# Stick-breaking attention on one core: z for a pair of heads at a time, one head in each half of the PE array's rows, in place of z for one head over all rows

## Chip, cores and metric

The kernel runs on one core of a Trainium2 chip. The metric is device time in microseconds (us) of one execution; the figure compared is the median of several runs, and one further execution is profiled.

## The reference

One layer of a streaming encoder trunk: 1024 tokens, width 1024, all in float32. It has three parts, each followed by a layer norm over `alpha*x + y`: self-attention, cross-attention into a memory of 256 tokens (4 heads), and a gated MLP with a short convolution. Only the first part matters here. It has 16 heads of width 64 and works on blocks of 128 queries:

```python
z = einsum('bhtd,bhsd->bhts', q[start:end], k[:end]) * 64 ** -0.5
earlier = arange(end)[None, :] < arange(start, end)[:, None]
log_keep = where(earlier, log_sigmoid(-z), 0.0)
csum = cumsum(log_keep, axis=-1)
w = where(earlier, exp(log_sigmoid(z) + csum[..., -1:] - csum), 0.0)
out = einsum('bhts,bhsd->bhtd', w, v[:end])
```

The output of the 16 heads is multiplied by a 1024 x 1024 matrix (`mix_wo`), added to `alpha*x` and normalized.

## The kernel before

**Numbers as pairs.** Every product is made to float32 accuracy from fp32r operands: each operand is split into hi (a cast) and lo (the rest, by a subtraction); `split` (L77) does that on two engines that its caller names. `mm3` (L100 to L103) makes a product as three matmuls, hi by hi, hi by lo, lo by hi, into one PSUM accumulator.

**PSUM.** Eight banks, two each under the tags acc (projections), pv, z and tp (L65 to L75).

**Projections.** x arrives transposed in eight tiles of 128 features and is split into xh and xl (L392 to L396). `proj_steps` (L182) is a generator: a step is one `mm3` of 512 columns. Head h takes one 128 x 1024 weight (`wqk`: 64 columns of q, 64 of k), two halves of 512 tokens, eight steps each; after it comes half of the values of a pair of heads (`wv`). `weights` (L164) loads a weight into wraw (two buffers) and splits it on POOL into whl (two buffers). The first head's queries and keys and the first pair's values are made ahead of the loop, as x arrives (L383 to L406).

**Queries and keys of a head.** `qk_out` (L131) copies the accumulator to pj on ACT, casts both halves on ACT into q1 (rows 0 to 63: hi of q) and k1 (rows 64 to 127: hi of k), subtracts the lo parts on POOL into the other halves of q1 and k1, and has two transfers on the SP queue build q2, which is q1 with its halves exchanged. So k1 holds lo over hi, q1 hi over lo and q2 lo over hi: q1 by k1 gives hi-lo and lo-hi, q2 by k1 gives lo-lo and hi-hi. Two 128-row matmuls thus make z.

**Attention.** `z_piece` (L207) makes a block of 128 queries by S = 128 to 1024 keys, in one or two pieces of at most 512 columns: two matmuls into a z bank (L215, L216), then a sigmoid on ACT into sig (L217); over the block one mask on POOL (L219) and one product scan on DVE (L222). `t_piece` (L224) transposes up to four 128 x 128 pieces of sig on TensorE into tp and splits them into wT (ACT and DVE). `pv_piece` (L236) multiplies wT by the differences of the values (vst); its lo part has 64 output columns. `o_piece` (L248) adds the ends and, for the odd head of a pair, sends two blocks of oT to DRAM (o_d) on the SP queue.

**Order.** `attention` (L266) takes half a head at a time ("quad": 18 of the 36 blocks). While the transposes and products of one quad are issued, the z pieces of the next are put between them in proportion, and `spend` (L271) draws steps of `other_steps` by a planned PE time: 24 steps per head, with an offset LEAD of -5, none within the last head. The compiler's scheduler then orders each engine's instructions by this program order as priority, among those it holds ready. `LAG` keeps three wT ahead of their products.

**What the other steps are.** After all projections, `other_steps` (L373) closes the pool of xh and xl, yields until the attention says that z of the last even head is under way, closes att3 (tiles of the even heads) and goes on with `mem_steps` (L340): mh and ml of the memory, then vacc (values of the memory, weights xv) and kacc (keys, weights xk), with the eight parts of `mix_wo` (wo, L365) loaded and split in between. xv and xk come into buffers of their own (xraw, two), wo and the memory into wraw. Then `out_ln` (L478) multiplies by wo (yacc) and normalizes; its residual tiles come from the pool rp, opened in `mem_steps`.

Of the kernel before, what the change touches and what calls it, by code (L numbers as in the profile page):

```python
# [27 lines left out]
P = 128  # L28
D = 1024
# [12 lines left out]
def trunk(ctx, tc, out, xT, xn, memT, wqk, wv, wo, xq, xk, xv, xo, up, cw, dn, lng, lnb):  # L42
# [80 lines left out]
    def qk_tiles(h):  # L123
        return [(att2 if h % 2 else att3).tile([P, T], R, name=f"{n}{h % 2}") for n in ("q1", "q2", "k1")]

    def evacuate(acc, n=512):
        pj = att.tile([P, 512], F32, name="pj", bufs=3)
        nc.scalar.copy(out=pj[:, :n], in_=acc)
        return pj[:, :n]

    def qk_out(qk, acc, ns):  # L131

        q1, q2, k1 = qk
        pj = evacuate(acc)
        for dst, r in ((q1, slice(0, 64)), (k1, slice(64, 128))):
            nc.scalar.copy(out=dst[r, ns], in_=pj[r])
        nc.gpsimd.tensor_tensor(out=q1[64:128, ns], in0=pj[0:64], in1=q1[0:64, ns].bitcast(F32), op=ALU.subtract)
        nc.gpsimd.tensor_tensor(out=k1[0:64, ns], in0=pj[64:128], in1=k1[64:128, ns].bitcast(F32), op=ALU.subtract)
        nc.sync.dma_start(out=q2[0:64, ns].bitcast(F32), in_=q1[64:128, ns].bitcast(F32))
        nc.sync.dma_start(out=q2[64:128, ns].bitcast(F32), in_=q1[0:64, ns].bitcast(F32))  # L140

    def v_out(pair, acc, n):
        vst, vend = pair
# [7 lines left out]
        dv = att.tile([P, 512], F32, name="pj", bufs=3)  # L151
# [20 lines left out]
    def vst_tile(pr):  # L172

        p = att2 if pr % 2 else att3
        return p.tile([P, KT, 2, 128], R, name=f"vst{pr % 2}"), p.tile([P, NTB], F32, name=f"vend{pr % 2}")

    heads = {}
    pairs = {}

    ready = {0}  # L180

    def proj_steps():  # L182

        for h in range(1, H):
            w = weights(wqk[h])
            qk = heads[1] if h == 1 else qk_tiles(h)
            for n, ns in halves():
                acc = acc_tile(name="qkacc")
                for kt in range(KT):
                    proj_part(w, acc, kt, ns)  # L190
                    yield
                qk_out(qk, acc, ns)
            heads[h] = qk
            ready.add(h)
            pr = (h + 1) // 2
            if pr < H // 2:
                n = 1 - h % 2
                w = weights(wv[pr])
                if n == 0:
                    pairs[pr] = pairs[1] if pr == 1 else vst_tile(pr)  # L200
                acc = acc_tile(name="vtacc")
                for kt in range(KT):
                    proj_part(w, acc, kt, slice(512 * n, 512 * n + 512))
                    yield
                v_out(pairs[pr], acc, n)

    def z_piece(h, i, sig):  # L207

        q1, q2, k1 = heads[h]
# [9 lines left out]
        nc.gpsimd.affine_select(out=sig[:, S - P:S], in_=sig[:, S - P:S], pattern=[[-1, P]], base=-1,  # L219
                                channel_multiplier=1, compare_op=ALU.is_ge, fill=1.0)  # L220
        kr = sig[:, :S][:, ::-1]
        nc.vector.tensor_tensor_scan(out=kr, data0=kr, data1=kr, initial=1.0, op0=ALU.mult, op1=ALU.bypass)  # L222
# [25 lines left out]
    def o_piece(h, d, pv):  # L248
        r = slice(64 * (h % 2), 64 * (h % 2) + 64)
        if h % 2 == 0 and d == 3:  # L250
            state["oT"] = att.tile([P, NTB, P], F32, name="oT", bufs=2)
# [10 lines left out]
    ATT_PE = 0.109 * 36 * 2 + 0.218 * 20  # L262
    LEAD = -5
    LAG = 3

    def attention(others):  # L266
        seq = [(h, q) for h in range(H) for q in (((3, 0), (2, 1)) if h < H - 1 else ((2, 1), (0, 3)))]
        clock = {"t": 0.0, "n": 0}
        pend = []

        def spend(dt):  # L271
            clock["t"] += dt
            if clock["t"] > (H - 1) * ATT_PE:
                return
# [4 lines left out]
        def z_steps(h, quad, sigs):  # L279
            while h not in ready:  # L280
                next(others)
                clock["n"] += 1
            sig = att.tile([P, 18 * P], F32, name="sig", bufs=2)
            c = 0
            for d in quad:
                for i in (2 * d, 2 * d + 1):
                    sigs[i] = sig[:, c:c + P * (i + 1)]
                    c += P * (i + 1)
                    z_piece(h, i, sigs[i])
                    yield 0.109 * (i + 1)  # L290

        def flush():
            h, d, b0, wT, pv = pend.pop(0)
            pv_piece(h, d, b0, wT, pv)
            if b0 == 2 * d:
                o_piece(h, d, pv)
            return 0.436

        def t_steps(h, quad, sigs):
            for d in quad:  # L300
                pv = None
                for b0 in range(0, 2 * d + 2, 2):
                    wT = t_piece(sigs, d, b0)
                    yield 0.109 * (4 if b0 < 2 * d else 3)
                    if pv is None:
                        pv = pv_tile((P, 2, P), name="pv")
                    pend.append((h, d, b0, wT, pv))
                    if len(pend) > LAG:
                        yield flush()

        spend(0.0)
        sigs = {}
        for dt in z_steps(*seq[0], sigs):
            spend(dt)
        for g, hq in enumerate(seq):
            nxt = {}
            zs = z_steps(*seq[g + 1], nxt) if g + 1 < len(seq) else iter(())
            tz = tt = 0.0
            for dt in t_steps(*hq, sigs):
                tt += dt  # L320
                spend(dt)
                while tz < tt * 18 / 34:
# [7 lines left out]
            if seq[min(g + 2, len(seq) - 1)][0] == H - 1:  # L330
# [9 lines left out]
    def mem_steps():  # L340
        mp = mem_c.enter_context(pool(name="memp", bufs=1, side="right", reuse_waits="tile"))
        wop = mem_c.enter_context(pool(name="wop", bufs=1, side="right", reuse_waits="tile"))
        state["rp"] = mem_c.enter_context(pool(name="rp", bufs=2, side="right", reuse_waits="tile"))
# [19 lines left out]
        for dq in range(KT):  # L363
            w = load_w(xk[dq], "pool", "pool", raw=mp.tile([P, 1024], F32, name="xraw", bufs=2)).rearrange("p a (k m) -> p a k m", k=KT)
# [17 lines left out]
    heads[0], heads[1], pairs[0], pairs[1] = qk_tiles(0), qk_tiles(1), vst_tile(0), vst_tile(1)  # L382
    w0, wv0 = [], []  # L383
    for k2 in range(KT // 2):
        for src, lst in ((wqk[0], w0), (wv[0], wv0)):
# [5 lines left out]
        for kt in (2 * k2, 2 * k2 + 1):  # L391
            xr = att.tile([P, 18 * P], F32, name="sig", bufs=2)  # L392
# [3 lines left out]
    w0, wv0 = (w[1].rearrange("p a (k m) -> p a k m", k=KT) for w in (w0, wv0))  # L396
    accs = [acc_tile(name="qkacc") for n in range(2)]
    vccs = [pv_tile(name="vtacc") for n in range(2)]
    for kt in range(KT):
        for w, cc in ((w0, accs), (wv0, vccs)):  # L400
            for n, ns in halves():
                proj_part(w, cc[n], kt, ns)
    for n, ns in halves():
        qk_out(heads[0], accs[n], ns)
    for n, ns in halves():
        v_out(pairs[0], vccs[n], n)  # L406
# [98 lines left out]
    att_c.close()  # L505
    h1c = ExitStack()
# [7 lines left out]
    with ExitStack() as c1:  # L514
        lnp = c1.enter_context(pool(name="ln1", bufs=1, side="right", reuse_waits="tile"))
        gb = load_ln(lnp, 0)
        for k, i in enumerate((4, 5, 2, 3, 0, 1, 6, 7)):
            out_ln(k, i, o_d, wts, xn, state["rp"], gb, h1_d, h1_evac)
# [489 lines left out]
```

## Time and profile before

| | |
|---|---|
| median of 3 runs | 1557.54 us (1556.81 to 1560.26) |
| the profiled execution | 1561.96 us |
| its span, first to last instruction | 1560.2 us |
| mean granted TensorE clock | 0.991 of full speed |
| PE, PEld busy | 1511.1 us (97%), 1261.4 us (81%) |
| DVE, ACT, POOL busy | 1090.8 us (70%), 701.6 us (45%), 676.9 us (43%) |
| instructions of PE | 7508 matmuls, 7508 weight loads |
| DMA | 191.00 MB, mean 122 GB/s |

Engines: PE is TensorE's matmul, PEld its weight load (which overlaps PE), DVE VectorE, ACT ScalarE, POOL GpSimd, SP SyncE, which here issues transfers. L215 is line 215. A share of busy time is a mean over stages with different limits, so a stage is read by itself. Matmuls are pipelined: one starts before the one ahead of it has ended, so the time that a matmul takes from its neighbours is the distance between starts. "a <-b" after an idle time names what ended it.

### The profile page before, as it was taken

The page shows a single profiled execution, that of the slowest core. Times are in us where ns is not written, and L with a number is a line of the kernel's source. Part 1 is how long each engine was busy: PE and PEld are TensorE (multiplying, and loading weights), DVE is VectorE, ACT ScalarE, POOL GpSimd, SP SyncE. Part 2 cuts the span into 40 slices and gives each one's busy share as a digit, 9 for nine tenths or more (in the row PEclk, how much of TensorE's full clock was granted, in tenths as well). Part 3 has the DMA queues.
Part 4 walks back from the last instruction along what each step waited for, and adds up shares of the span by engine and source line. Part 5 has one row for each costly group of instructions (what it writes and reads, how often), then busy time and mean ns, then how long its engine had stood idle before and what let it go on. Part 6 is the DMA issues. An engine that isn't in the chain of part 4 may idle for free.

```text
span 1560.2 us, 21007 instructions
## 1 busy us (share of the span) xinstructions
PE 1511.1 (97%) x7508; PEld 1261.4 (81%) x7508; DVE 1090.8 (70%) x1504; ACT 701.6 (45%) x1309; POOL 676.9 (43%) x627
## 2 busy tenths in 40 slices
PE   7999999999988999999999989999999999989997
PEld 5888888888877888888888867888888888778876
DVE  3466666676769836645437899777777777868896
ACT  4455565565567522123332355444444444444551
POOL 4775566556558730255401253222444543501042
PEclk9999999999998999999999999999999999999999
DMA  5322222122236443334234415443466662944631
GB/s 172 85 59 65 65 56 70 48 62 68 61 97 191 163 137 135 113 118 128 82 109 168 135 65 174 147 154 126 133 151 149 151 146 96 355 142 160 195 105 61
DMA packets 95352, 191.00 MB, mean 122 GB/s; under 512 B 11408, under 2 KB 33040, under 8 KB 95248
## 3 DMA queue, kind: packets, MB, share of 16 engines
q1 hardware_dynamic: 75760, 143.52, 29.2%
q0 software_dynamic: 11136, 27.27, 7.4%
q10 hardware_dynamic: 8352, 18.88, 3.6%
q8 instruction: 59, 0.97, 0.3%
q14 instruction: 45, 0.37, 0.1%
HBM read 146.63 MB, written 57.67 MB: 131 GB/s over the span
## 4 chain that ended last, share of the span: by engine, by line
PE 81%; DVE 6%; POOL 5%; issue 3%; DMA 3%; ACT 1%; SPq 0%; POOLq 0%; DVEq 0%; ACTq 0%
PE yacc L101 4%; PE yacc L102 4%; PE yacc L103 4%; PE qkacc L101 4%; PE qkacc L103 4%; PE qkacc L102 4%; PE mb L101 3%; PE mb L103 3%; PE mb L102 3%; PE tp L231 3%; PE y L102 3%; PE y L103 3%; PE y L101 3%; PE mc L102 2%; PE mc L103 2%
## 5 line engine op out<-in xcount | busy, mean ns | idle before, releaser
L222 DVE TENSOR_TENSOR_SCAN sig<-sig 128x896 f32<-128x896 f32 (+7 forms) x128 | 196.4, 1541 | 75.5 <-POOL sig L219 56.5
L87 POOL TENSOR_TENSOR whl<-wraw,whl 128x512 fp32r<-128x512 f32 (+2 forms) x97 | 172.7, 1791 | 134.2 <-ACT whl L79 132.7
L85 DVE TENSOR_TENSOR wT<-tp,wT 128x512 fp32r<-128x512 f32 (+1 forms) x160 | 98.8, 628 | 63.1 <-ACT wT L79 61.9
L79 ACT CAST whl<-wraw 128x512 fp32r<-128x512 f32 (+3 forms) x113 | 82.3, 739 | 123.7 <-PE y L103 39.1
L79 ACT CAST wT<-tp 128x512 fp32r<-128x512 f32 (+1 forms) x160 | 86.5, 546 | 105.4 <-PE tp L231 102.0
L448 POOL TENSOR_TENSOR rs<-rs,mhalf 128x1 f32<-128x1 f32 x24 | 22.3, 930 | 224.5 <-DVE rs L447 224.5
L217 ACT ACTIVATE sig<-z 128x384 f32<-128x384 f32 (+2 forms) x192 | 92.1, 495 | 49.9 <-PE z L216 48.8
L219 POOL TENSOR_SCALAR_AFFINE_SELECT sig<-sig 128x128 f32<-128x128 f32 x128 | 60.2, 474 | 119.7 <-ACT sig L217 112.0
L101 PE MATMUL qkacc<-xh,whl 128*128 128x512 f32 x256 | 103.2, 403 | 8.0 <-ACT xh L79 6.5
L101 PE MATMUL mb<-b_t,ws 128*128 128x512 f32 x264 | 104.7, 397 | 2.0 <-ACT b_t L79 1.0
L102 PE MATMUL y<-whl,aop 128*128 128x512 f32 x264 | 103.7, 393 | 1.1 <-DVE whl L85 1.0
L103 PE MATMUL mb<-b_t,ws 128*128 128x512 f32 x264 | 103.9, 394 | 0.0
L103 PE MATMUL qkacc<-xh,whl 128*128 128x512 f32 x256 | 102.0, 400 | 1.9 <-POOL whl L87 1.9
L102 PE MATMUL mb<-b_t,ws 128*128 128x512 f32 x264 | 103.3, 391 | 0.0
L102 PE MATMUL qkacc<-xl,whl 128*128 128x512 f32 x256 | 102.3, 399 | 0.0
L103 PE MATMUL yacc<-wo,whl 128*128 128x512 f32 x256 | 100.8, 394 | 0.0
L102 PE MATMUL yacc<-wo,whl 128*128 128x512 f32 x256 | 100.8, 394 | 0.0
L101 PE MATMUL yacc<-wo,whl 128*128 128x512 f32 x256 | 100.4, 393 | 0.3 <-ACT whl L79 0.3
L103 PE MATMUL y<-whl,aop 128*128 128x512 f32 x264 | 99.7, 391 | 0.0
L79 ACT CAST ws<-wt 128x512 fp32r<-128x512 f32 x88 | 54.5, 621 | 99.3 <-PE mb L103 53.9
L231 PE MATMUL tp<-ident,sig 128*128 128x128 f32 x576 | 89.4, 275 | 8.8 <-DVE wT L85 8.8
L83 POOL TENSOR_SCALAR whl<-wraw 128x512 fp32r<-128x512 f32 (+2 forms) x74 | 55.3, 760 | 88.3 <-PE qkacc L103 31.3
(222 smaller groups left out, 4393.9 us busy)
## 6 DMA issues: line engine op xcount, KB each, us to landing
wraw<-in_up SPq DMA_DIRECT2D x22, 512.0 KB, 3.6
wr<-in_up SPq DMA_DIRECT2D x22, 512.0 KB, 3.6
u_d<-in_dn SPq DMA_DIRECT2D x44, 256.0 KB, 5.5
float<-g_d POOLq DMA_DIRECT2D x44, 256.0 KB, 6.4
wraw<-u_d SPq DMA_DIRECT2D x44, 256.0 KB, 2.9
g_d<-gate SPq DMA_DIRECT2D x20, 512.0 KB, 2.9
q<-q SPq DMA_DIRECT2D x64, 128.0 KB, 2.2
h_d<-r SPq DMA_DIRECT2D x32, 256.0 KB, 2.1
```

The costliest lines, as they stand in the source:

```text
L79: nc.scalar.copy(out=hi, in_=src)
L83: nc.gpsimd.tensor_scalar(out=hi, in0=src, scalar1=1.0, scalar2=0.0, op0=ALU.mult, op1=ALU.add)
L85: nc.vector.tensor_tensor(out=lo, in0=src, in1=hi.bitcast(F32), op=ALU.subtract)
L87: nc.gpsimd.tensor_tensor(out=lo, in0=src, in1=hi.bitcast(F32), op=ALU.subtract)
L101: nc.tensor.matmul(o, lhsT=lh, rhs=rh, start=first, stop=False, skip_group_check=more)
L102: nc.tensor.matmul(o, lhsT=lh, rhs=rl, start=False, stop=False, skip_group_check=more)
L103: nc.tensor.matmul(o, lhsT=ll, rhs=rh, start=False, stop=last, skip_group_check=more)
L217: nc.scalar.activation(out=sig[:, a:b], in_=z[:, :b - a], func=AF.Sigmoid, scale=-0.125)
L219: nc.gpsimd.affine_select(out=sig[:, S - P:S], in_=sig[:, S - P:S], pattern=[[-1, P]], base=-1, channel_multiplier=1, compare_op=ALU.is_ge ...
L222: nc.vector.tensor_tensor_scan(out=kr, data0=kr, data1=kr, initial=1.0, op0=ALU.mult, op1=ALU.bypass)
L231: nc.tensor.transpose(out=tp[:, k], in_=sigs[2 * d + u][:, P * j:P * j + P], identity=ident)
L448: nc.gpsimd.tensor_tensor(out=rs, in0=rs, in1=mhalf, op=ALU.pow)
```

## The change

`qk_tiles`, `qk_out`: for a pair of heads there are now four tiles, q hi, q lo, k hi, k lo, each with the even head in rows 0 to 63 and the odd head in rows 64 to 127. The weights are cut accordingly (`wq`, `wk`: 128 columns for a pair). The accumulator is split straight from PSUM by ACT and DVE. `z_piece` makes the pieces of both heads together: hi by hi, hi by lo, lo by hi, each as two matmuls of 64 rows, one per head, into the two z banks; then two sigmoids, and for each head a mask and a scan.

```diff
     def qk_out(hl, acc, ns):
-        q1, q2, k1 = qk
-        pj = evacuate(acc)
-        for dst, r in ((q1, slice(0, 64)), (k1, slice(64, 128))):
-            nc.scalar.copy(out=dst[r, ns], in_=pj[r])
-        nc.gpsimd.tensor_tensor(out=q1[64:128, ns], in0=pj[0:64], in1=q1[0:64, ns].bitcast(F32), op=ALU.subtract)
-        nc.gpsimd.tensor_tensor(out=k1[0:64, ns], in0=pj[64:128], in1=k1[64:128, ns].bitcast(F32), op=ALU.subtract)
-        nc.sync.dma_start(out=q2[0:64, ns].bitcast(F32), in_=q1[64:128, ns].bitcast(F32))
-        nc.sync.dma_start(out=q2[64:128, ns].bitcast(F32), in_=q1[0:64, ns].bitcast(F32))
+        split(acc, hl[0][:, ns], hl[1][:, ns])
...
+        rows = slice(0, 64), slice(64, 128)
         for (a, b) in reversed([(0, c), (c, S)] if c < S else [(0, S)]):
-            z = z_tile()
-            nc.tensor.matmul(z[:, :b - a], lhsT=q1[:, tb], rhs=k1[:, a:b], start=True, stop=False)
-            nc.tensor.matmul(z[:, :b - a], lhsT=q2[:, tb], rhs=k1[:, a:b], start=False, stop=True)
-            nc.scalar.activation(out=sig[:, a:b], in_=z[:, :b - a], func=AF.Sigmoid, scale=-0.125)
+            zs = [z_tile() for r in rows]
+            for n, (x, y) in enumerate(((0, 0), (0, 1), (1, 0))):
+                for z, r in zip(zs, rows):
+                    nc.tensor.matmul(z[:, :b - a], lhsT=q[x][r, tb], rhs=k[y][r, a:b], start=n == 0, stop=n == 2)
+            for z, sig in zip(zs, sigs):
+                nc.scalar.activation(out=sig[:, a:b], in_=z[:, :b - a], func=AF.Sigmoid, scale=-0.125)
...
+    Z_PE, T_PE, V_PE = 0.171, 0.109, 0.436
+    QUAD_PE = 18 * Z_PE + 2 * (18 * T_PE + 5 * V_PE)
+    FIRST, PACE = 40, 25
...
-            while clock["n"] < LEAD + 24 * clock["t"] / ATT_PE:
-                clock["n"] += 1
-                next(others, None)
+            while clock["n"] < FIRST + PACE * clock["t"] / QUAD_PE:
+                other()
...
-        state["rp"] = mem_c.enter_context(pool(name="rp", bufs=2, side="right", reuse_waits="tile"))
...
-                w = load_w(xv[n, k2], "act", "pool", raw=mp.tile([P, 1024], F32, name="xraw", bufs=2)).rearrange("p a (k m) -> p a k m", k=2)
+                w = load_w(xv[n, k2], "act", "pool").rearrange("p a (k m) -> p a k m", k=2)
...
-            w = load_w(xk[dq], "pool", "pool", raw=mp.tile([P, 1024], F32, name="xraw", bufs=2)).rearrange("p a (k m) -> p a k m", k=KT)
+            w = load_w(xk[dq], "pool", "pool").rearrange("p a (k m) -> p a k m", k=KT)
```

Around it:

- A quad is now 18 blocks of both heads of a pair (16 quads in all, before 32 of one head). `proj_steps` makes, per pair, the values after queries and keys; the first pair's values are no longer made ahead of the loop but its queries and keys are, and 40 other steps are drawn over the first quad's z, then 25 per quad, to the end.
- A product waits in the program for the values of its pair (`v_ready`).
- The tiles of queries and keys alternate by pair between att3 and att2; the values' tiles all lie in att2, so att3 closes once z of the last but one pair is made.
- Buffers: sig 4 (before 2, now two per quad), pj 2 (3), oT 1 (2). The buffers xraw are gone: xv and xk come into wraw. The pool rp is opened after the attention's pools are closed.

## Rows read from the trace of the kernel before

**Rows 1.** The page's first line.
```profile
span 1560.2 us, 21007 instructions
```
**Rows 2.** Windows: length, then busy time (count) by engine, PE clock, DMA share, GB/s.
```profile
0.00:31.00 31.00, 24.45 (x95) 19.46 (x96) 11.97 (x17) 11.89 (x19) 11.62 (x23) 1.00 0.63 203
31.00:60.00 29.00, 26.11 (x110) 20.14 (x109) 6.34 (x7) 13.62 (x27) 25.05 (x27) 0.94 0.31 78
60.00:460.00 400.00, 397.68 (x2321) 343.85 (x2320) 264.31 (x309) 225.97 (x510) 237.04 (x266) 1.00 0.23 64
460.00:563.00 103.00, 89.96 (x584) 79.42 (x583) 83.53 (x78) 62.52 (x124) 81.66 (x52) 0.95 0.56 178
563.00:1560.00 997.00, 972.91 (x4407) 798.50 (x4405) 724.63 (x1094) 387.58 (x631) 321.57 (x261) 0.99 0.46 139
```
**Rows 3.** Waits of PE, 60 to 460 us: total us, times, longest.
```profile
PE tp L231 <- DVE wT L85: 1.4, 2, 0.8
PE qkacc L101 <- DVE pj L152: 0.9, 1, 0.9
```
**Rows 4.** Timeline of PE, 203 to 205 us: start, duration, instruction.
```profile
203.20 0.34 PE L216 MATMUL z<-k,q 128*128 128x384 f32 x1
203.38 0.28 PE L244 MATMUL pv<-wT,vst 128*128 128x256 f32 x1
...
204.18 0.39 PE L215 MATMUL z<-k,q 128*128 128x512 f32 x1
204.41 0.39 PE L216 MATMUL z<-k,q 128*128 128x512 f32 x1
204.63 0.28 PE L244 MATMUL pv<-wT,vst 128*128 128x256 f32 x1
204.75 0.28 PE L246 MATMUL pv<-wT,vst 128*64 128x256 f32 x1
204.87 0.40 PE L101 MATMUL qkacc<-xh,whl 128*128 128x512 f32 x1
```
**Rows 5.** The same view, 213 to 214 us.
```profile
213.64 0.22 PE L215 MATMUL z<-k,q 128*128 128x128 f32 x1
213.70 0.28 PE L216 MATMUL z<-k,q 128*128 128x128 f32 x1
```
**Rows 6.** Groups by form, ACT, 0 to 455 us: busy us, mean ns | idle before.
```profile
L217 ACT ACTIVATE sig<-z 128x512 f32<-128x512 f32 x68 | 40.3, 602 | 11.0 <-PE z L216 10.6
...
L136 ACT CAST q<-pj 64x512 fp32r<-64x512 f32 x30 | 17.6, 622 | 2.3 <-PE z L215 2.1
```
**Rows 7.** The same view for POOL.
```profile
L138 POOL TENSOR_TENSOR k<-pj,k 64x512 fp32r<-64x512 f32 x30 | 51.6, 1730 | 1.8
...
L137 POOL TENSOR_TENSOR q<-pj,q 64x512 fp32r<-64x512 f32 x30 | 42.1, 1414 | 12.2 <-ACT q L136 9.1 <-issue 1.9
```
**Rows 8.** The same view for DVE.
```profile
L152 DVE TENSOR_TENSOR pj<-vT,vtacc 128x512 f32<-128x512 f32 x16 | 11.0, 687 | 15.6 <-POOL k L138 10.2 <-ACT vT L149 5.2
```
**Rows 9.** Timeline of PE, 35 to 36 us; in brackets the idle time before.
```profile
35.60 0.50 PE L103 MATMUL qkacc<-xh,whl 128*128 128x512 f32 x1 [0.88 <-POOL whl L87]
```
**Rows 10.** DMA issues, 450 to 566 us: size of each, median us to landing.
```profile
xraw<-in_xv SPq DMA_DIRECT2D x8, 512.0 KB, 4.5
wraw<-in_wo SPq DMA_DIRECT2D x8, 512.0 KB, 3.7
xraw<-in_xk SPq DMA_DIRECT2D x8, 512.0 KB, 4.6
...
o_d<-oT SPq DMA_DIRECT2D x16, 64.0 KB, 3.5
```
**Rows 11.** Groups by form, 455 to 563 us.
```profile
L87 POOL TENSOR_TENSOR whl<-xraw,whl 128x1024 fp32r<-128x1024 f32 x16 | 43.3, 2707 | 7.7 <-ACT whl L79 7.0
L85 DVE TENSOR_TENSOR wo<-wraw,wo 128x1024 fp32r<-128x1024 f32 x8 | 17.3, 2164 | 0.1
...
L79 ACT CAST wo<-wraw 128x1024 fp32r<-128x1024 f32 x8 | 8.4, 1049 | 2.1 <-DMA wraw<-in_wo 1.9
```

More of the change, by code (lines that the diff above doesn't have):

```diff
@@ L39, with trunk @@
 EPS = 1e-5
-def trunk(ctx, tc, out, xT, xn, memT, wqk, wv, wo, xq, xk, xv, xo, up, cw, dn, lng, lnb):
+def trunk(ctx, tc, out, xT, xn, memT, wq, wk, wv, wo, xq, xk, xv, xo, up, cw, dn, lng, lnb):
     nc = tc.nc
@@ L172, in vst_tile @@
     def vst_tile(pr):
[L174 to L180, printed above, removed]
-    def proj_steps():
-        for h in range(1, H):
-            w = weights(wqk[h])
-            qk = heads[1] if h == 1 else qk_tiles(h)
+        return (att2.tile([P, KT, 2, 128], R, name=f"vst{pr % 2}"), att2.tile([P, NTB], F32, name=f"vend{pr % 2}"))
+    qks, pairs = {}, {}
+    ready, v_ready = {0}, set()
+    def proj_steps():
+        for pr in range(H // 2):
+            if pr:
+                qks[pr] = qk_tiles(pr)
+                for src, hl in zip((wq, wk), qks[pr]):
+                    w = weights(src[pr])
+                    for n, ns in halves():
+                        acc = acc_tile(name="qkacc")
+                        for kt in range(KT):
+                            proj_part(w, acc, kt, ns)
+                            yield
+                        qk_out(hl, acc, ns)
+                ready.add(pr)
+            w = weights(wv[pr])
+            pairs[pr] = vst_tile(pr)
             for n, ns in halves():
-                acc = acc_tile(name="qkacc")
+                acc = acc_tile(name="vtacc")
                 for kt in range(KT):
@@ L191, in proj_steps, with z_piece @@
                     yield
[L192 to L204, printed above, removed]
                 v_out(pairs[pr], acc, n)
-    def z_piece(h, i, sig):
-        q1, q2, k1 = heads[h]
+            v_ready.add(pr)
+    def z_piece(pr, i, sigs):
+        q, k = qks[pr]
         tb = slice(P * i, P * i + P)
@@ L249, in o_piece @@
         r = slice(64 * (h % 2), 64 * (h % 2) + 64)
-        if h % 2 == 0 and d == 3:
-            state["oT"] = att.tile([P, NTB, P], F32, name="oT", bufs=2)
+        if state.get("pair") != h // 2:
+            state["pair"] = h // 2
+            state["oT"] = att.tile([P, NTB, P], F32, name="oT", bufs=1)
         vend = pairs[h // 2][1]
@@ L260, in o_piece, with other, z_steps @@
                 nc.sync.dma_start(out=o_d[i][:, h // 2], in_=state["oT"][:, i])
-    ATT_PE = 0.109 * 36 * 2 + 0.218 * 20
-    LEAD = -5
+    Z_PE, T_PE, V_PE = 0.171, 0.109, 0.436
+    QUAD_PE = 18 * Z_PE + 2 * (18 * T_PE + 5 * V_PE)
+    FIRST, PACE = 40, 25
     LAG = 3
     def attention(others):
-        seq = [(h, q) for h in range(H) for q in (((3, 0), (2, 1)) if h < H - 1 else ((2, 1), (0, 3)))]
+        seq = [(pr, q) for pr in range(H // 2) for q in (((3, 0), (2, 1)) if pr < H // 2 - 1 else ((2, 1), (0, 3)))]
         clock = {"t": 0.0, "n": 0}
         pend = []
+        def other():
+            clock["n"] += 1
+            next(others, None)
         def spend(dt):
             clock["t"] += dt
-            if clock["t"] > (H - 1) * ATT_PE:
-                return
-            while clock["n"] < LEAD + 24 * clock["t"] / ATT_PE:
-                clock["n"] += 1
-                next(others, None)
[L279 to L283, printed above, removed]
+            while clock["n"] < FIRST + PACE * clock["t"] / QUAD_PE:
+                other()
+        def z_steps(pr, quad, sigs):
+            while pr not in ready:
+                other()
+            tiles = [att.tile([P, 18 * P], F32, name="sig", bufs=4) for hh in range(2)]
             c = 0
@@ L286, in z_steps @@
                 for i in (2 * d, 2 * d + 1):
-                    sigs[i] = sig[:, c:c + P * (i + 1)]
+                    for hh in range(2):
+                        sigs[hh][i] = tiles[hh][:, c:c + P * (i + 1)]
                     c += P * (i + 1)
-                    z_piece(h, i, sigs[i])
-                    yield 0.109 * (i + 1)
+                    z_piece(pr, i, [sigs[hh][i] for hh in range(2)])
+                    yield Z_PE * (i + 1)
         def flush():
             h, d, b0, wT, pv = pend.pop(0)
+            while h // 2 not in v_ready:
+                other()
             pv_piece(h, d, b0, wT, pv)
@@ L296, in flush, with t_steps @@
                 o_piece(h, d, pv)
[L297 to L316, printed above, removed]
+            return V_PE
+        def t_steps(pr, quad, sigs):
+            for hh in range(2):
+                for d in quad:
+                    pv = None
+                    for b0 in range(0, 2 * d + 2, 2):
+                        wT = t_piece(sigs[hh], d, b0)
+                        yield T_PE * (4 if b0 < 2 * d else 3)
+                        if pv is None:
+                            pv = pv_tile((P, 2, P), name="pv")
+                        pend.append((2 * pr + hh, d, b0, wT, pv))
+                        if len(pend) > LAG:
+                            yield flush()
+        sigs = {}, {}
+        for k, dt in enumerate(z_steps(*seq[0], sigs)):
+            while clock["n"] < FIRST * (k + 1) / 4:
+                other()
+        for g, pq in enumerate(seq):
+            nxt = {}, {}
             zs = z_steps(*seq[g + 1], nxt) if g + 1 < len(seq) else iter(())
             tz = tt = 0.0
-            for dt in t_steps(*hq, sigs):
+            for dt in t_steps(*pq, sigs):
                 tt += dt
                 spend(dt)
-                while tz < tt * 18 / 34:
+                while tz < tt * 0.42:
                     dz = next(zs, None)
@@ L329, in attention @@
                 spend(dz)
[L330 removed]
+            if seq[min(g + 2, len(seq) - 1)][0] == H // 2 - 1:
                 state["att3 done"] = True
@@ L379, in other_steps @@
         yield from mem_steps()
-    heads[0], heads[1], pairs[0], pairs[1] = qk_tiles(0), qk_tiles(1), vst_tile(0), vst_tile(1)
-    w0, wv0 = [], []
+    qks[0] = qk_tiles(0)
+    w0, w1 = [], []
     for k2 in range(KT // 2):
-        for src, lst in ((wqk[0], w0), (wv[0], wv0)):
+        for src, lst in ((wq[0], w0), (wk[0], w1)):
             cs = slice(2 * P * k2, 2 * P * k2 + 2 * P)
@@ L395, in trunk @@
                 split(xr[:, ns], xh[:, kt, ns], xl[:, kt, ns])
-    w0, wv0 = (w[1].rearrange("p a (k m) -> p a k m", k=KT) for w in (w0, wv0))
-    accs = [acc_tile(name="qkacc") for n in range(2)]
-    vccs = [pv_tile(name="vtacc") for n in range(2)]
+    w0, w1 = (w[1].rearrange("p a (k m) -> p a k m", k=KT) for w in (w0, w1))
+    accs = [acc_tile(name="qkacc") for n in range(2)], [pv_tile(name="qkacc") for n in range(2)]
     for kt in range(KT):
-        for w, cc in ((w0, accs), (wv0, vccs)):
+        for w, cc in zip((w0, w1), accs):
             for n, ns in halves():
                 proj_part(w, cc[n], kt, ns)
[L403 to L406, printed above, removed]
+    for hl, cc in zip(qks[0], accs):
+        for n, ns in halves():
+            qk_out(hl, cc[n], ns)
     state = {"att3 done": False}
@@ L505, in trunk @@
     att_c.close()
+    rp1 = mem_c.enter_context(pool(name="rp", bufs=2, side="right", reuse_waits="tile"))
     h1c = ExitStack()
@@ L517, in trunk @@
         for k, i in enumerate((4, 5, 2, 3, 0, 1, 6, 7)):
-            out_ln(k, i, o_d, wts, xn, state["rp"], gb, h1_d, h1_evac)
+            out_ln(k, i, o_d, wts, xn, rp1, gb, h1_d, h1_evac)
     mem_c.close()
```

25 lines of the change are left out of this document (14 added, 11 removed).

## Prediction

> **What bounds the kernel now.** The page's first line gives the span, 1560.2 us [rows 1]; the execution it belongs to took 1561.96 us, 1.8 us lie around the span, and the median of the runs is 1557.54 us, 4.4 us less. I sum against the profiled execution and move the same difference to the median.
>
> The windows come next, because the change touches only the self-attention [rows 2]. See five stretches. In 0 to 31 us x arrives and is split. In 31 to 60 us the first head is made ready: PE is busy 26.11 of 29 us at a granted clock of 0.94. From 60 to 460 us projections and attention run together: PE 397.68 of 400 us, DVE 264, ACT 226, POOL 237; TensorE alone is the bound. From 460 to 563 us the last three heads run beside the memory steps: PE 89.96 of 103 us, clock 0.95, DVE 83.53, POOL 81.66; here PE waits. The 997 us after that hold nothing the diff edits except where one small pool is opened.
>
> A busy PE need not be a PE at its peak, so I read who it waited for: in 60 to 460 us 2.3 us in all, two entries [rows 3]. So a matmul microsecond removed there is a microsecond of the kernel.
>
> The price of a matmul is the distance between two starts, not its duration [rows 4, 5]: 512 columns 0.23 us (204.18, 204.41, 204.63), 384 columns 0.18 (203.20, 203.38), 256 columns 0.12 (204.63, 204.75), 128 columns 0.06 (213.64, 213.70). The duration of the 512-wide one, 0.39 us, is 0.16 longer than that distance: the tail of one lies under the next.
>
> **Part 1, z by 64-row matmuls.** For one head z_piece makes 12 pieces (5 of 512 columns, 3 of 384, 3 of 256, 1 of 128), two matmuls each. One pass over them costs 5 x 0.231 + 3 x 0.176 + 3 x 0.119 + 0.058 = 2.10 us (the third digit is the mean over the stretch; with the two digits of the rows it is 2.11), so 16 heads x 2 passes = 67.1 us. Afterwards each pair makes three passes for two heads. If the two halves of the rows run side by side, 8 pairs x 3 passes x 2.10 = 50.4 us: **-16.8**. If they run one after the other it is six passes, 100.7 us: +33.6. No row of this trace has a matmul of fewer than 128 rows. The nearest is the product with 64 columns (128*64), which follows and precedes full ones at the ordinary distance of 0.12 us [rows 4], so a partly used array costs nothing extra in itself. I take side by side, since the two operands lie in different rows and the results in different banks.
>
> The Trainium skill (TensorE: Matmul & The Clock Gate, Measured speedup vs the span model) gives 3.07 times for four 32-row tiles of 512 columns, 77% of the ideal. By that share z would cost 65.5 us, an estimate from that page, and the sum below would be +3.7 instead of -11.4; no run here shows it.
>
> Weights: every matmul loads its own 128 columns. At 128 wide the distance is 0.06 us with a load in each [rows 5], so a couple of loads can't take less than about 0.12, and the one 128-wide piece gains nothing from lying side by side: 3 x 0.058 x 8 = **+1.4** (0 to 1.4). Wider pieces cover two loads.
>
> Banks: z has two PSUM banks. Before, one piece filled one, and the next piece had the other. Now one pair of pieces fills both, and the next pair waits for two sigmoids, which ACT does one after the other, 0.602 us at 512 wide [rows 6]. Four of the 12 pieces are the second half of a block over 512 columns and come right behind the first. PE need not stand still, since projections are ready, but head A's bank is free 0.6 us before B's, so A's matmuls may be put ahead of B's and the two no longer lie beside each other. One lost overlap per such piece costs a pass: (0.176 + 3 x 0.231) x 8 = **+7.0**; none lost 0, all three lost +20.9. I take one, since 0.6 us is under three passes of 0.23.
>
> **Part 2, queries and keys split from PSUM.** Gone, 32 times: the copy to pj stays as the copy to hi, but two half copies on ACT (0.62 each), two subtractions on POOL (1.41 and 1.73) and two transfers on SP go; one subtraction on DVE comes, near 0.687, the row that also reads PSUM [rows 6 to 8]. ACT loses some 40 us, POOL 100, SP 64 issues, DVE gains 22. All of it lies under PE in 60 to 460 us, where DVE goes from 264 to some 285 of 400. On the path: **0**. Bounds: -2.3, all PE waits of rows 3; +4, if the bank that DVE now frees 0.69 us later than ACT did is missed in one of five of the 28 halves. What waits on DVE behind such a subtraction is the lo split of wT, and on that PE's transposes.
>
> One oT instead of two adds a wait: the first add of the next pair on DVE waits for o_d to be written, 3.5 us from issue to landing [rows 10]. Between the adds lie four pv pieces; a head has ten and takes some 30 us (176 matmuls and transposes of the 2321 in 400 us), so 12 us cover it. Cost 0; uncovered, it would hold the same lo splits.
>
> **Part 3, start.** POOL no longer does q and k between the two halves of the second weights, for whose lo part PE stood 0.88 us [rows 9]. In 31 to 60 us 2.9 us are idle and 6% of clock is missing, 1.7 us: at most -4.6. The first split of the new weights still waits for the buffers, so I take **-3** (-4.6 to 0).
>
> **Part 4, end.** As before, the memory steps can begin when the last but one pair's z is made, with three heads to go; that moment moves with what parts 1 and 3 save. But xv and xk lose their own raw buffers and share two wraw buffers with wo. A buffer is held from issue until split: xv 4.5 + 1.0 + 2.7, xk 4.6 + 1.0 + 2.7, wo 3.7 + 1.0 + 2.2 us [rows 10, 11] (xk's cast on POOL taken like ACT's). Eight of each, over two buffers: 8 x 23.4 / 2 = 94 us, in a stretch of 103. It fits by 9 us. Against that, POOL has no q and k of the last heads, and wo's subtractions no longer crowd in ahead of the scans on DVE. I take **0**, between -13 (all idle time of PE there) and +12 (each of 24 turns 1 us later). The residual's buffers open later; r is needed only after 48 yacc matmuls, 11 us, so 0.
>
> **Sum:** -16.8 + 1.4 + 7.0 + 0 - 3 + 0 = -11.4. Profiled execution 1550.6, median **1546**.
>
> **Rivals.**
> - **A, the forecast**: 1546, own range 1530 to 1556. For: PE is the bound for 400 us. Against: no 64-row matmul in the trace. Chance 0.64.
> - **B, slower: PE empties at each change between whole and halved rows.** Some 12 groups a pair go in and out: 192 changes. What a full emptying could cost is the tail that now lies under the next matmul, 0.16 us [rows 4]: +31, 1577. It decides from 11.4 / 192 = 59 ns. Against: between full and 64-column matmuls no such cost stands in the rows. 0.10. The Trainium skill (TensorEngine Tiling (Array Packing), Key Properties) says that a change of tiling mode drains the engine; if 128x64 is such a mode, rows 4 speak against the cost, and for 64 rows no run here shows it yet.
> - **C, slower: the halves run one after the other.** z +33.6 in place of -8.4, start -3: +31, 1588. It is also the case that the change doesn't do what it says. 0.06.
> - **D: all overlap lost in the second halves.** +13.9 on the forecast: +2.5, 1560. For: both sigmoids are on one queue. 0.10.
> - **E: the wraw turns bind the end.** +12: 1558. For: only 9 us of room. Against: POOL is freer. 0.10.
>
> **How the numbers follow.** A difference of 0.2%, 3.1 us, is about what a measurement of this kernel can tell from no change. A is faster: 0.64. D and E are within it, less a little that lies beyond: 0.17. B, C and that rest: 0.19. The range leaves out C, B beyond 135 ns per change, and the corner where z keeps all its overlap and the end loses most of its idle time: 1526 to 1572.
>
> **What would show it.** Right: three z lines of 64 rows, 576 matmuls in all, starts of a couple a few ns apart and 0.23 us from couple to couple; 60 us to the last projection shorter by some 9 us; POOL under half busy there; yacc starting near 551 us. Wrong: couples 0.46 us apart (C); a gap of over 60 ns before and after each group (B); three matmuls of one head in a row (D); PE or vacc and kacc waiting for wraw transfers, with the stretch after the last projection over 110 us (E).

## The result: 2.7% slower

The changed kernel takes a median of 1600.19 us (1596.29 to 1602.88, four runs), the kernel before 1557.57 us in the same comparison: ratio 1.0269, 95% interval 1.0239 to 1.0298, or +42.6 us. The forecast was 1546, its range ended at 1572. The profiled execution took 1596.29 us (before 1561.96); it is the lowest of the four, so the windows below hold 34.3 us of the loss.

The page's first lines of the kernel after:

```profile
span 1594.5 us, 20976 instructions
...
PE 1550.1 (97%) x7700; PEld 1254.9 (79%) x7700; DVE 1097.5 (69%) x1536; ACT 667.3 (42%) x1245; POOL 537.6 (34%) x535
```

POOL lost 139 us of work and PE gained 39 us of busy time. The windows of after, cut at the last projection (480 us) and at the first yacc (598 us), with the columns of [rows 2]:

```profile
0.00:31.00 31.00, 24.31 (x98) 19.88 (x99) 14.78 (x20) 13.20 (x21) 13.82 (x26) 1.00 0.62 204
31.00:60.00 29.00, 29.00 (x138) 21.30 (x137) 13.68 (x12) 10.03 (x21) 14.79 (x18) 1.00 0.17 55
60.00:480.00 420.00, 420.00 (x2406) 326.74 (x2405) 264.87 (x328) 193.04 (x446) 118.54 (x184) 1.00 0.11 32
480.00:598.00 118.00, 103.08 (x658) 86.55 (x656) 78.77 (x84) 63.85 (x128) 69.16 (x48) 0.94 0.49 156
598.00:1594.00 996.00, 973.74 (x4404) 800.45 (x4404) 725.37 (x1095) 387.15 (x631) 321.32 (x261) 0.99 0.45 140
```

Against [rows 2]: the start is better, as forecast (31 to 60 us: 29.00 busy at clock 1.00, before 26.11 at 0.94). Yacc begins at 598 us instead of 563, and the rest is as long as before (996 and 997 us). So the loss lies between 60 and 598 us. And in 60 to 480 us PE is busy for all of 420.00 us at full clock, and no wait is listed there: most of the loss is inside a PE that counts as busy, and no view of waits can show it.

It shows in the distance between starts. The timeline of PE in after (x2: two matmuls that start together, one per head, which is a couple; z matmuls with no other matmul between them are a group):

```profile
204.39 0.39 PE L102 MATMUL vtacc<-xl,whl 128*128 128x512 f32 x1
204.62 0.40 PE L103 MATMUL vtacc<-xh,whl 128*128 128x512 f32 x1
204.94 0.50 PE L208 MATMUL z<-kh,qh 64*128 64x512 f32 x2
205.28 0.39 PE L208 MATMUL z<-kl,qh 64*128 64x512 f32 x2
205.50 0.39 PE L208 MATMUL z<-kh,ql 64*128 64x512 f32 x2
205.82 0.38 PE L238 MATMUL pv<-wT,vst 128*128 128x256 f32 x1
206.04 0.28 PE L240 MATMUL pv<-wT,vst 128*64 128x256 f32 x1
206.16 0.28 PE L238 MATMUL pv<-wT,vst 128*128 128x256 f32 x1
```

By [rows 4] 512 columns take 0.23 us from start to start and 256 take 0.12. Read down: 0.32 into the first couple (0.09 too much), 0.34 to the second (0.11), 0.22 to the third (as it should be), 0.32 to the first full matmul (0.09), 0.22 behind 256 columns (0.10), then 0.12 again. The couples do lie side by side, and inside the group their price is that of one matmul. But each passage between 128-row and 64-row matmuls costs twice, once ahead of the first instruction of the new kind and once behind it. The medians over the groups that stand beside no transpose (some 90 of 125) are 96 + 105 ns going in and 94 + 107 ns going out, **0.40 us for a group**; the same measure on the kernel before gives at most 3 ns.

The weight loads show what is lost. The timeline of PEld, after, same place:

```profile
204.39 0.19 PEld L103 LDWEIGHTS vtacc<-xh,whl 128*128 128x128 f32 x1
204.94 0.19 PEld L208 LDWEIGHTS z<-kh,qh 64*128 64x128 f32 x2 [0.36 <-ACT wT L79]
205.05 0.19 PEld L208 LDWEIGHTS z<-kl,qh 64*128 64x128 f32 x2
205.28 0.19 PEld L208 LDWEIGHTS z<-kh,ql 64*128 64x128 f32 x2
205.82 0.19 PEld L238 LDWEIGHTS pv<-wT,vst 128*128 128x128 f32 x1 [0.35 <-issue]
```

The load for the matmul at 204.62 is made at 204.39, under the matmul ahead. The first 64-row load is not made until 204.94, when the 0.23 us of the last full matmul are over, and so again on the way out at 205.82. (The ACT named beside the 0.36 had ended at 204.83. It is not what the load stood for: where such a cast is named, 14 times, the matmul comes 94 ns late in the median, and where none is named, 49 times, 91 ns.) In the kernel before, the load for z at 204.18 comes at 204.06, under its neighbour:

```profile
204.06 0.19 PEld L215 LDWEIGHTS z<-k,q 128*128 128x128 f32 x1
204.18 0.19 PEld L216 LDWEIGHTS z<-k,q 128*128 128x128 f32 x1
```

A second thing shows in the order on PE: 96 groups of three couples became 125. 71 are whole, 33 are one head's three matmuls alone, the others are fragments; 226 of the 288 couples lie side by side. One such lone head, timeline of PE in after:

```profile
226.76 0.40 PE L101 MATMUL qkacc<-xh,whl 128*128 128x512 f32 x1
227.09 0.49 PE L208 MATMUL z<-kh,qh 64*128 64x512 f32 x1
227.42 0.39 PE L208 MATMUL z<-kl,qh 64*128 64x512 f32 x1
227.66 0.39 PE L208 MATMUL z<-kh,ql 64*128 64x512 f32 x1
227.98 0.51 PE L102 MATMUL qkacc<-xl,whl 128*128 128x512 f32 x1
```

It pays the passage in and out (0.33 and 0.32 instead of 0.23) and has nothing beside it. That is the broken overlap of rival D, with B's price on top.

### The profile page after: what moved, and what is told of

It reads as the page before. It is cut to its first block, busy times and chain, and to the rows that moved or that the text cites. A ratio compares the mean times of both kernels' runs of the same rounds, so it can differ in the third digit from the quotient of the medians.

```text
span 1594.5 us, 20976 instructions
## 1 busy us (share of the span) xinstructions
PE 1550.1 (97%) x7700; PEld 1254.9 (79%) x7700; DVE 1097.5 (69%) x1536; ACT 667.3 (42%) x1245; POOL 537.6 (34%) x535
## 4 chain that ended last, share of the span: by engine, by line
PE 83%; DVE 5%; DMA 4%; POOL 4%; issue 2%; ACT 1%; SPq 0%; POOLq 0%; ACTq 0%; DVEq 0%
PE z L208 5%; PE qkacc L101 4%; PE qkacc L102 4%; PE qkacc L103 4%; PE tp L225 4%; PE yacc L101 4%; PE yacc L102 4%; PE yacc L103 4%; PE mb L101 3%; PE mb L103 3%; PE mb L102 3%; PE y L102 3%; PE y L103 3%; PE y L101 2%; PE pv L238 2%; PE mc L101 2%
## 5 line engine op out<-in xcount | busy, mean ns | idle before, releaser
L87 POOL TENSOR_TENSOR whl<-wraw,whl 128x1024 fp32r<-128x1024 f32 (+2 forms) x99 | 192.0, 1950 | 145.6 <-ACT whl L79 144.3
L216 DVE TENSOR_TENSOR_SCAN sig<-sig 128x1024 f32<-128x1024 f32 (+7 forms) x128 | 183.5, 1460 | 50.3 <-ACT sig L210 36.0
L79 ACT CAST whl<-wraw 128x512 fp32r<-128x512 f32 (+3 forms) x121 | 90.5, 760 | 132.7 <-PE yacc L103 40.9
L210 ACT ACTIVATE sig<-z 128x384 f32<-128x384 f32 (+3 forms) x192 | 86.5, 490 | 100.9 <-PE z L208 99.9
L213 POOL TENSOR_SCALAR_AFFINE_SELECT sig<-sig 128x128 f32<-128x128 f32 x128 | 46.2, 373 | 214.5 <-ACT sig L210 213.8
L83 POOL TENSOR_SCALAR whl<-wraw 128x512 fp32r<-128x512 f32 (+2 forms) x68 | 64.9, 966 | 138.6 <-PE qkacc L103 53.2
```

Source lines behind the costliest of these rows:

```text
L79: nc.scalar.copy(out=hi, in_=src)
L83: nc.gpsimd.tensor_scalar(out=hi, in0=src, scalar1=1.0, scalar2=0.0, op0=ALU.mult, op1=ALU.add)
L87: nc.gpsimd.tensor_tensor(out=lo, in0=src, in1=hi.bitcast(F32), op=ALU.subtract)
```

## The experiments

Two theories were set against each other first. **Theory 1**: overlap is real, and the passages between row counts eat it (with groups broken up, since the two banks come free one at a time). **Rivals**: the halves don't overlap; or the loss comes from another part, the new start, the split from PSUM or the shared raw buffers. All ratios are against the kernel before.

**e1: z with full rows, two matmuls per head, all else as changed.** The sums of both heads land in each bank and one of the three products is missing.

```diff
-            for n, (x, y) in enumerate(((0, 0), (0, 1), (1, 0))):
+            for n, (x, y) in enumerate(((0, 0), (1, 0))):
...
-nc.tensor.matmul(z[:, :b - a], lhsT=q[x][r, tb], rhs=k[y][r, a:b], start=n == 0, stop=n == 2)
+nc.tensor.matmul(z[:, :b - a], lhsT=q[x][:, tb], rhs=k[y][:, a:b], start=n == 0, stop=n == 1)
```

> The changed kernel with z made over all 128 rows again, in two passes per head (hi by hi and lo by hi; both heads' rows are summed and hi by lo is left out, so z has other values). All else stays: layout, split from PSUM, order of the steps, buffers. Theory 1, the price lies at the change between 128-row and 64-row matmuls (each group of z stands 0.39 us longer than its columns ask for, 125 groups): z falls from some 98 us to 67, so about 30 us less than the changed kernel, 1565 to 1572, and what is left above the kernel before, some 10 us, is the end with the shared raw buffers. Theory 2, the new order of steps and the buffers cost the time and z is no dearer: within 10 us of the changed kernel, 1590 to 1603.

Measured 1551.40 us, ratio 0.9949 (0.9930 to 0.9969). So **z alone costs 48.8 us** (1600.19 - 1551.40), and all other parts together gain 7.7 (1551.40 against 1559.11 before, same chip). What "z alone" holds besides the passages comes out with e2. Windows of e1:

```profile
31.00:60.00 29.00, 29.00 (x136) 23.99 (x135) 13.39 (x14) 10.00 (x22) 13.62 (x23) 1.00 0.17 55
60.00:437.00 377.00, 375.15 (x2164) 324.00 (x2163) 253.99 (x311) 181.52 (x422) 112.26 (x175) 1.00 0.11 35
437.00:552.00 115.00, 103.47 (x706) 92.53 (x704) 90.53 (x97) 70.56 (x148) 75.47 (x53) 0.99 0.44 143
```

Yacc begins at 552.2, before at 563.1: 10.9 us. The windows account for 10.1 of it: in 31 to 60 us 2.9 us of idle and 1.7 us of missing clock are gone (4.6); in the end stretch idle falls from 13.0 to 11.5 us and the missing clock from 5% of 103 to 1% of 115 us (together 5.5).

**e2: the same with all three products**, so against the changed kernel only the rows differ (the sums of both heads again land in each bank).

```diff
-nc.tensor.matmul(z[:, :b - a], lhsT=q[x][r, tb], rhs=k[y][r, a:b], start=n == 0, stop=n == 2)
+nc.tensor.matmul(z[:, :b - a], lhsT=q[x][:, tb], rhs=k[y][:, a:b], start=n == 0, stop=n == 2)
```

> As the run with two passes over 128 rows, but three passes per head, six full matmuls per pair of pieces (both heads' rows summed, so z has other values). No change of row count, no overlap. Theory 1: 33 us above the run with two passes, about 1600, so overlap with its changes buys as much as it costs against six plain passes. Theory 2 (TensorE is not what binds): under 15 us above it.

Measured 1594.97 us (two runs), ratio 1.0229 (1.0188 to 1.0270), 43.6 us above e1, where 16 more passes of 2.10 make 33.6. The other 10 are waits: from 60 us to the first yacc idle time and missing clock are 25.2 us, in e1 14.5. The window, and the first yacc on the timeline of PE in e2:

```profile
475.00:595.00 120.00, 99.63 (x660) 89.33 (x658) 76.81 (x84) 63.32 (x128) 68.61 (x48) 0.96 0.48 154
```

```profile
595.36 0.79 PE L101 MATMUL yacc<-wo,whl 128*128 128x512 f32 x1 [6.14 <-ACT whl L79]
```

This run has no passage, so such waits at the end (22.0 us in after) are not made by passages, though they are part of the 48.8. With the matmuls in the same order as after it takes nearly the same time: what lying side by side saves, the passages take back in full.

**e3: both heads on rows 0 to 63**, so that nothing can lie side by side (the odd head gets the even head's z).

```diff
-lhsT=q[x][r, tb], rhs=k[y][r, a:b]
+lhsT=q[x][0:64, tb], rhs=k[y][0:64, a:b]
```

> The changed kernel with both matmuls of each couple on rows 0 to 63 (the odd head gets the even head's z). The changes of row count stay, the overlap goes. If the couples of the changed kernel really overlap (starts 3 to 5 ns apart), 226 couples lose about 0.17 us each: 35 to 45 us above the changed kernel, 1635 to 1645, starts of a couple one matmul apart. If the starts are only recorded close together and the array works them off in turn: the same time as the changed kernel.

Measured 1634.70 us (two runs), ratio 1.0484 (1.0447 to 1.0521), 34.5 above after. The overlap is real: at their widths (72 of 512 columns, 66 of 384, 66 of 256, 22 of 128) the 226 couples are 37.4 us. The timeline of PE in e3 (x2: here two that follow each other):

```profile
201.34 0.50 PE L208 MATMUL z<-kh,qh 64*128 64x256 f32 x2
201.68 0.40 PE L208 MATMUL z<-kl,qh 64*128 64x256 f32 x2
201.91 0.40 PE L208 MATMUL z<-kh,ql 64*128 64x256 f32 x2
202.24 0.33 PE L240 MATMUL pv<-wT,vst 128*64 128x256 f32 x1
```

Couples of 256 columns stand 0.23 apart, twice the 0.12 that they take in after (200.73 to 200.85 us there). C is out.

**e4: the kernel before, its two z matmuls cut to rows 0 to 63.** No pair, no couple, no other part of the change: the passage alone. z holds only half of each product.

```diff
-lhsT=q1[:, tb], rhs=k1[:, a:b]
-lhsT=q2[:, tb], rhs=k1[:, a:b]
+lhsT=q1[0:64, tb], rhs=k1[0:64, a:b]
+lhsT=q2[0:64, tb], rhs=k1[0:64, a:b]
```

> The kernel before with z's two matmuls on rows 0 to 63 only (half of each product is left out, so z has other values). Number, columns and order of the matmuls are those of before; only the row count changes. Theory 1: each of the some 170 separate groups of z now pays about 0.2 us on the way in and 0.2 us on the way out: 60 to 75 us slower, 1617 to 1632, with weight loads of z starting only when the matmul before has drained. Theory 2, a change of row count costs nothing: 1557.

Measured 1616.63 us (two runs), ratio 1.0368 (1.0324 to 1.0412): **+57.5 us for the same number of columns**. Timeline of PE in e4:

```profile
300.48 0.40 PE L101 MATMUL qkacc<-xh,whl 128*128 128x512 f32 x1
300.81 0.32 PE L215 MATMUL z<-k,q 64*128 64x128 f32 x1
300.97 0.27 PE L216 MATMUL z<-k,q 64*128 64x128 f32 x1
301.18 0.50 PE L102 MATMUL qkacc<-xl,whl 128*128 128x512 f32 x1
301.51 0.39 PE L103 MATMUL qkacc<-xh,whl 128*128 128x512 f32 x1
```

0.33 in place of 0.23, 0.16 in place of 0.06, 0.33 in place of 0.23 at the end. There are 198 groups, 79 us at 0.40, so 0.29 us of each reaches the total; from 31 us to the first yacc the idle time of PE fell from 18.2 [rows 2] to 8.2 us, so part of the price was paid by waits that had been there. The other 12 us are not traced.

**e5: the couple's two banks as one tile**, so that both come free together (z's banks have a pool of their own for it, which is opened anew after the attention).

```diff
-            zs = [z_tile() for r in rows]
+            z2 = zpool[0].tile([P, 2, 512], F32, name="z", tag="z", bufs=1)
+            zs = [z2[:, 0], z2[:, 1]]
...
```

> The changed kernel with the two z banks of a pair of pieces as one tile, so that both become free together. In the order of TensorE's instructions z then stands in 98 groups instead of 125, 94 of them whole (six matmuls), and nearly all 288 couples lie side by side instead of 226. Theory 1 (each group costs about 0.3 us of entering and leaving, each lost couple one matmul of some 0.175 us): 27 x 0.31 + 62 x 0.175 = 19 us less than the changed kernel, 1577 to 1588, still above the kernel before, since 96 groups cost about 30 us and the overlap gives back 17. Rival, broken groups are the whole of the loss: at or below the kernel before, 1558. Rival, they don't matter: 1596 to 1603.

Measured 1574.69 us, ratio 1.0103 (1.0084 to 1.0121): 25.5 us of the loss are gone. The order on PE now has 98 groups, 94 whole, 287 of 288 couples side by side. Windows of e5:

```profile
60.00:455.00 395.00, 394.20 (x2343) 313.22 (x2342) 260.23 (x317) 182.84 (x428) 114.44 (x183) 1.00 0.11 34
455.00:575.00 120.00, 106.51 (x714) 90.48 (x713) 88.64 (x94) 68.96 (x145) 73.49 (x52) 0.93 0.45 141
```

With its one tile z must wait for both sigmoids, and still PE is idle for only 0.8 us of 395: projections fill in, as the prediction said. What remains against e1 is 23.3 us; -16.8 of overlap, +1.4 and 98 groups of 0.40 make 23.8. That agrees in part by luck, as the measured sum below shows.

**e6: an own raw buffer for xk** (rival E), in the changed kernel.

```diff
-load_w(xk[dq], "pool", "pool")
+load_w(xk[dq], "pool", "pool", raw=mp.tile([P, 1024], F32, name="xraw"))
```

> The changed kernel with one raw buffer of its own for xk, so that xk and wo no longer take turns in wraw. Theory: the stretch from the last projection to the first yacc, 118 us, was set by these turns (8.5 us for each of eight xk): it falls by about 1.3 us each, 10 us in all: 1588 to 1592. Rival, the stretch is set by the attention's own chain: under 3 us less.

The reason to try it is the chain of waits in after, which runs through xk's turns (start, us, what):

```profile
542.06 3.58 DMA wraw<-in_xk
...
545.78 2.02 POOL whl L83
...
547.88 2.38 POOL whl L87
550.28 3.68 DMA wraw<-in_xk
...
554.12 1.07 POOL whl L83
...
555.26 4.21 POOL whl L87
559.49 3.43 DMA wraw<-in_xk
```

Measured 1602.50 us, ratio 1.0277 (1.0262 to 1.0293): a miss, no gain. The chain then runs through wo instead, whose subtractions come early and stand among the scans on DVE. Chain of waits in e6:

```profile
533.85 2.59 DVE sig L216
...
536.93 1.23 DVE wo L85
...
541.08 5.49 DMA wraw<-in_wo
...
547.04 3.93 DVE sig L216 x2
550.97 1.13 DVE wo L85
```

PE's waits for the lo split of wT rise there from 4.5 to 11.1 us. One wait was exchanged for another.

**e7 to e10: which other part gains, and is there a version that beats both?** Each puts one part of the change into the kernel before: e7 the start (queries and keys of heads 0 and 1 ahead of the loop, the first values after, guarded by v_ready, LEAD 11); e8 the same with wo's loads held behind xk's in the program's order; e9 the split straight from PSUM; e10 is e9 and e7 together. The core of e7 and of e9:

```diff
-        for src, lst in ((wqk[0], w0), (wv[0], wv0)):
+        for src, lst in ((wqk[0], w0), (wqk[1], wv0)):
...
-        pj = evacuate(acc)
-            nc.scalar.copy(out=dst[r, ns], in_=pj[r])
-        nc.gpsimd.tensor_tensor(out=q1[64:128, ns], in0=pj[0:64], in1=q1[0:64, ns].bitcast(F32), op=ALU.subtract)
+            nc.scalar.copy(out=dst[r, ns], in_=acc[r])
+        nc.vector.tensor_tensor(out=q1[64:128, ns], in0=acc[0:64], in1=q1[0:64, ns].bitcast(F32), op=ALU.subtract)
```

> The kernel before with the changed kernel's order of the start: queries and keys of the first two heads are made as x arrives, the first pair's values come as the first of the other steps. z stays as before. Theory: the start gives what the changed kernel gained between 31 and 60 us, 3 to 4 us: 1553 to 1555. Rival, it is given back at the end: 1557.

> As the run with the other start, and each load of wo is issued only behind the load of xk that precedes it in the program, so that wo's subtractions no longer come in a bunch ahead of the scans on DVE at the start of the end stretch. Theory: PE's waits there (3.8, 3.0 us and smaller ones, and the lower clock after each) shrink: 4 to 8 us below the run with the other start, 1546 to 1550. Rival, wo comes too late for yacc: above it.

> The kernel before with queries and keys split straight from PSUM: two casts on ACT from the accumulator, two subtractions on DVE in place of those on POOL, no copy to pj; the two transfers to q2 stay, z stays at two passes over 128 rows. Theory, taking q and k off POOL is what makes the run with two passes 8 us faster than the kernel before (POOL stood in the way at the start, where PE waited for the lo part of the second weights, and at the end, where POOL worked on q and k of the last heads while the memory's weights waited): 1551 to 1555. Rival, the 8 us come from the order of the steps and the buffers: 1557 to 1560.

> As the run before it, and with the queries and keys of the first two heads made at the start and the first pair's values as the first other steps. Theory: with q and k off POOL the new start gives the 4 us between 31 and 60 us that the run with the start alone did not show (PE was busy 26.4 of 29 us there): 1547 to 1552. Rival, what the start gives is lost again at the end, as in the run with the start alone: 1555 or more.

All four missed. e7: 1564.24 us, ratio 1.0033 (1.0021 to 1.0046); PE still waits 2.09 us for POOL in 31 to 60 us, with POOL busy for 28.02 of 29 us there, now with the queries and keys of two heads. e8: 1563.85 us, 1.0026 (1.0017 to 1.0035). e9: 1595.91 us, **1.0246** (1.0228 to 1.0264). e10: 1590.20 us, 1.0206 (1.0190 to 1.0221). The waits of PE in e9, 60 to 498 us (total us, times, longest), and the window:

```profile
PE vtacc L101 <- DVE k L137: 8.2, 5, 2.3
PE tp L230 <- DVE wT L85: 4.8, 4, 1.2
PE pv L243 <- ACT wT L79: 4.4, 5, 1.0
```

```profile
60.00:498.00 438.00, 418.03 (x2325) 354.36 (x2324) 298.07 (x364) 211.50 (x489) 141.13 (x211) 0.96 0.20 55
```

PE stands still for 20.0 us of the window: 8.2 for accumulator banks that DVE has not yet read, the scans being on the same queue, and most of the rest for the splits of wT, the lo half of which has to get past the same subtractions. The granted clock of the window is 0.96, which is 17.5 us more. Together 37.5, in before 2.3 from 60 us to its last projection; yacc begins 34.5 us later than in before. So the split from PSUM is not free in every surrounding. In the changed kernel it is: no wait of PE stands in 60 to 480 us. There one subtraction of 128 rows serves two heads, in e9 two of 64 rows serve each; that this is the difference that counts was not tried.

**e11 and e12: the kernel before without its rule that nothing is drawn within the last head**; e12 also with LEAD 24, so that projections run further ahead.

```diff
-            if clock["t"] > (H - 1) * ATT_PE:
-                return
...
-    LEAD = -5
+    LEAD = 24
```

> The kernel before, whose attention goes on drawing other steps during its last head, as the changed kernel does. Theory, the 8 us that the run with two passes gains over the kernel before come in part from memory steps drawn beside the last heads: 1552 to 1556. Rival, the scheduler takes ready memory steps there anyway, and the program's order of them changes little: 1556 to 1560.

> As the run before it, with the other steps drawn 29 steps earlier (LEAD 24 in place of -5), which is nearer to the changed kernel's 40 ahead of the first quad's products. Theory, the earlier end of the projections (437 us in the run with two passes, 456 in the kernel before) is what gains: the last projection comes 5 to 15 us earlier and the time is 1550 to 1555. Rival, the steps are bound by their buffers and the lead is lost at once: 1556 to 1560.

e11: 1558.79 us, ratio 0.9999 (0.9990 to 1.0008). e12: 1578.57 us, 1.0124 (1.0102 to 1.0145); its last projection started at 464.7 us, in before at 455.6, so not earlier. Neither gains; that rule is not what made e1 faster.

## Why the prediction was wrong, point by point

**The step that failed: passages between whole and halved rows cost nothing.** The prediction took the 64-column products [rows 4] as nearest row: "a partly used array costs nothing extra in itself". They half-use the array's columns, not its rows, and they are as cheap in after (0.12 us at 206.04). They say nothing of rows. Rival B named the mechanism, and then priced and counted it too low: at most 0.16 us (the tail that lies under the next matmul) for each of 192 passages. Measured: 0.20 for each, since the instruction behind the first one is late too, and 250 passages; some 41 us of that reach the time (below), where the sum had 0. It had a chance of 0.10; its own bound of 59 ns was passed more than three times over.

The Trainium skill (TensorEngine Tiling (Array Packing), Key Properties) says that switching the tiling mode drains the engine. The traces agree for 64-row matmuls, at 0.20 us a switch (e4, and after), and show none for 128x64. The rule was read and dismissed on the wrong row.

**Banks, +7.0: mechanism right, size off.** Overlap was lost as forecast, because head A's bank comes free first; the forecast was one couple in three of the second pieces, 32 couples, at most 20.9 us. By the order on PE 62 couples were parted, at their widths (47 of 512 columns, 6 of 384, 7 of 256, 2 of 128) 12.9 us. Some 35 of them are in second pieces, near the forecast, though there a few pieces lost nearly all three; the others are in first and single pieces, which the term had left out. It also left out that a broken group pays two more passages: 29 groups more, 11.7 us. e5 took both away and got 25.5 back.

**Overlap, -16.8, and the 128-wide couples, +1.4: right.** The two of a couple start 4 ns apart in the median; inside a group 512-wide couples stand 0.22 to 0.23 us from the next, 128-wide ones 0.11, near the 0.12 that two loads were priced at. The Trainium skill (TensorE: Matmul & The Clock Gate, Measured speedup vs the span model) gives 3.07 times for four 32-row tiles, 77% of the ideal; inside a group of two tiles here nothing is missing (0.22 against 0.23), and the loss lies at its edges.

**Start, -3: right in its place** (4.6 us in e1's window, the whole of the bound). e7 shows that the order alone doesn't bring it while POOL has the lo parts to make.

**Split from PSUM, 0: right here**, in after and in e1, though e9 shows that the +4 put as its upper bound is no bound in another surrounding.

**End, 0:** e1's end stretch gained 5.5 us of idle and clock, after's did not (14.9 us idle, clock 0.94), nor did e2's. Rival E's turns do stand on the chain, some 8.2 us for each xk (533.79 to 582.69 for six), but e6 took them away and gained nothing. The sign named for E, over 110 us from the last projection to yacc, could not tell: before has 107.5 there, and e1, which gains, 115.

**The sum as measured**, from e1 to after: -16.8 + 1.4 + 125 x 0.402 + 12.9 = +47.8. The start of yacc moved from 552.2 to 598.1, 45.9; the median by 48.8. That these agree so well is partly luck, since the sum leaves out the idle time and missing clock from 60 us to the first yacc: 22.0 us in after, 14.5 in e1, 22.7 in e5. With them, 40.9 us are left for the passages in after (45.9 + 16.8 - 1.4 - 12.9 - 7.5): 0.33 us of a group's 0.40 reaches the time, and 0.31 in e5.

**What stays open.** That the other parts gain some 8 us is shown by e1; which of them does it is read from windows only, since e7 to e12 didn't reproduce it in the kernel before. What makes the longer waits at the end of after and e2 is not settled either. e1 is no full computation, and of those that are, none was faster than the kernel before. Groups longer than three couples, which would have fewer edges, were not tried: z has two banks, and the other six are in use.

## What to carry to other kernels

Before cutting a matmul's rows to run two side by side, count the groups that would stand between full-row matmuls and set 0.3 to 0.4 us for each against what its overlap saves; a group of three 512-wide couples in place of four full matmuls saves 0.23 us and loses. If it must be done, give a couple's accumulators as one tile, so that the scheduler can't part them. And a nearest row must share the dimension that is changed: one that halves the columns is no price for halving the rows.

## What the runs showed of the hardware that was not expected

- The passage between 128-row and 64-row fp32r matmuls costs 96 + 105 ns in and 94 + 107 ns out. The first weight load of the new kind is not made under the matmul ahead, and the matmul behind the first one is late by as much again.
- A matmul of 64 output columns among full ones costs none of that, and two 64-row matmuls in different halves of the rows overlap fully (e3: on the same half not at all).
- PE shows as busy through these passages (420.00 of 420 us), so a busy share, a granted clock of 1.00 and an empty list of waits together are still no proof that PE was at its peak.
